# A gated delta rule in chunks of 128 frames: roots finished on GpSimd, the query's output part scaled out of PSUM, the identity by TensorE, Silu for the query, a tile of their own for the step sizes

## The chip, the cores and the metric

The kernel runs on one core of a Trainium2 chip. Five engines work side by side, each in the order of its own instruction list: PE (TensorE, matrix products), DVE (VectorE), ACT (ScalarE), POOL (GpSimd) and SP (SyncE, which issues transfers). An instruction that waits for a semaphore holds up all that stand behind it on its engine. The metric is the device time of one execution, in microseconds.

## The reference, cut to what matters

One layer of a streaming trunk: RMS norm, one input projection, a gated-delta-rule group of 4 heads (128 x 128 state each) beside an S5 state-space group, both gated, one output projection, a final norm. It runs on 4096 prompt frames from zero state and on 32 sample frames that continue a cache. What the change touches is the delta-rule group:

```python
    q = l2_normalize(q) * (DN_DK ** -0.5)        # q, k, v = silu(conv(h @ w_in))
    k = l2_normalize(k)                          # x * rsqrt(sum(x * x) + 1e-6)
    beta = sigmoid(b_logit)
    ...
    lower = where(strict, (k * beta) @ k.T * decay, 0.0) + eye     # one chunk of frames
    u = triangular_solve(lower, v * beta)
    w = triangular_solve(lower, k * beta * exp(gc))
    attn = where(incl, q @ k.T * decay, 0.0)
    ...
        v_new = u_b - w_b @ S                                      # the scan over chunks
        o = (q_b * exp(gc_b)) @ S + attn @ v_new
        S = S * exp(g_last) + (k_b * exp(g_last - gc_b)).T @ v_new
    ...
    o_dn = rms_norm(o_dn, dn_norm_w) * silu(z_dn)
```

`gc` is the running sum of the logarithm of the decay within a chunk, `beta` the step size.

## The kernel before

The time falls into stages. Up to some 690 us the kernel norms the frames, projects the S5 input, runs the S5 blocks and the gate projections, and makes the tables of decays. To 930 us it prepares weights and the first block of queries, keys and values. From there to some 2070 us it runs the delta rule beside the dense work of that stage, and from there to the end the output projection.

The delta-rule stage takes chunks of 128 frames, 32 of the prompt and one of the sample. PE's program is put together by a small planner (`Drive`): one stream of dense work (`qkv`, 256 frames at a time, line 1352 and around; then `s5out`) has the lowest priority, and four streams of chunks, `chunk(ci, ...)`, yield to one another and to it after each step with an estimate of how long the step's operands take. The lists of the other engines are then set by a scheduler that goes by estimated times, so each list is fixed before the kernel runs. A chunk's buffers carry the number of its stream, as in `br0` to `br3`, so that a buffer comes free with the end of the chunk four places before.

A chunk has three parts.

- The front, held by one chunk at a time (`busy`): PE transposes keys to rows, ACT squares them into `sk` (1522), POOL adds epsilon (1525), `rsqrt` makes the inverse root: a power on POOL (129), then one Newton step in three instructions on DVE (130 to 132), `rq_k` and `rqt_k`. ACT scales the keys to `kn` (1529). POOL makes `kd` from the keys and a table of decays (1546), multiplies the step sizes with the decay matrix, `br` times `dm` (1548), and the queries with `gr`, the exponential of `gc` for each frame (1550). `br` and `gr` come from DRAM, each frame's value repeated on all 128 partitions, by SP's transfers of lines 1510 and 1507. DVE scales the key products with `br` into `at` (1560) and the query products with `dm` (1571). `pair` splits a float32 tile into a float16 high half (ACT, 1482) and the rest (POOL or DVE, 1483), and `mm3` makes a product of two such pairs by three matmuls.
- The inverse of the triangular matrix (`inverse`, two slots): blocks of 4, 8, 16, 32 and 64 frames, `T`, `T64`, `Tf`, by small products on PE with DVE and ACT between them, then one residual correction: `e` is the identity less the product of matrix and `Tf` (1742, DVE), split into `eh` (1744, ACT) and `el` (1746, POOL).
- The chain through the state: `sp` (the state's pair), the corrected values `vn`, the output `po` as the sum of two products, query by state and attention by `vn`, in one PSUM bank, the state update `S_p` (1614, DVE), squares of `po` into `so` (1522, ACT; 1622, DVE), its inverse root `rq_o` with a factor `sdn` (1624), the gated output `o` from PSUM (1630, DVE, four heads), and its halves in `m16`, which lies in `dm` (1633, 1634).

In `qkv` the convolution is four multiplies into `acc` (1352 on ACT, 1354 on DVE); keys and values of all blocks but the first go through Silu (1356), queries through Tanh (1359) and (tanh + 1) times `acc` on DVE (1360).

## Time and profile before

| quantity | value |
| --- | --- |
| median of 3 runs | 2460.18 us (2457.91 to 2461.07) |
| profiled execution | 2456.1 us, its span 2454.4 us |
| PE busy in the span | 2080.0 us (85%) |
| DVE | 1578.9 us (64%) |
| ACT | 1204.6 us (49%) |
| POOL | 892.4 us (36%) |
| granted PE clock, mean | 0.937 |

The span is the part of the profiled execution from its first to its last instruction. The durations in the trace belong to that one execution. An engine is busy while an instruction runs on it; a wait is idle time and names the work that ended it.

### The profile page before, as it was taken

How to read it: one execution, taken by the hardware profiler on the slowest of the kernel's cores; microseconds unless marked ns; L12 is line 12 of the kernel's file. 1: busy time of each engine (PE TensorE's matmuls, PEld its weight loads, DVE VectorE, ACT ScalarE, POOL GpSimd, SP SyncE). 2: the span in 40 equal slices, each digit the busy share in tenths (PEclk: the TensorE clock that was granted, in tenths of full speed). 3: DMA queues.
4: the chain of work that ended last, by engine and by line, in shares of the span. 5: the costliest groups of instructions: out<-in, count | busy, mean ns of one | idle time of the engine just before them, and what ended most of it. 6: DMA issues, size and time to landing. Idle time of an engine off the chain costs nothing.

```text
span 2454.4 us, 47429 instructions
## 1 busy us (share of the span) xinstructions
PE 2080.0 (85%) x18040; PEld 1491.3 (61%) x18040; DVE 1578.9 (64%) x3715; ACT 1204.6 (49%) x3518; POOL 892.4 (36%) x1057
## 2 busy tenths in 40 slices
PE   3968898967799996986988789888878866999998
PEld 2635676734576554875777677777677743554443
DVE  3885766756474224886888778887878786642222
ACT  5457456423593113656666566666656564421101
POOL 1363011011102014556555555655655455420000
PEclk9989999979899997998999999999999888999999
DMA  5469877367864555231342233333333256455552
GB/s 164 152 165 248 164 164 183 67 75 104 233 174 125 116 123 112 57 80 40 79 83 69 62 66 85 76 83 76 62 58 58 58 143 123 117 142 155 152 146 90
DMA packets 458005, 278.05 MB, mean 113 GB/s; under 512 B 345112, under 2 KB 412928, under 8 KB 457264
## 3 DMA queue, kind: packets, MB, share of 16 engines
q1 hardware_dynamic: 435024, 206.94, 40.0%
q0 software_dynamic: 18000, 59.43, 7.3%
q10 hardware_dynamic: 4752, 8.65, 1.0%
q8 instruction: 141, 2.31, 0.4%
q14 instruction: 88, 0.72, 0.1%
HBM read 110.99 MB, written 86.23 MB: 80 GB/s over the span
## 4 chain that ended last, share of the span: by engine, by line
PE 32%; DVE 22%; DMA 15%; issue 14%; POOL 7%; ACT 6%; SPq 3%; POOLq 0%; DVEq 0%; ACTq 0%
PE pp L48 17%; PE pz L503 7%; DMA br<-be_d 6%; PE bk L48 4%; DVE acc L1354 3%; DMA gyt<-gy_d 2%; DMA h_d<-hl 2%; SPq L911 1%; DVE ubd L1687 1%; DMA gy_d<-vv 1%; DVE vv L879 1%; POOL br L1548 1%; PE bk L52 1%; PE pp L511 1%; DVE vv L885 1%
## 5 line engine op out<-in xcount | busy, mean ns | idle before, releaser
L503 PE MATMUL pz<-wz,hz 128*128 128x512 f16 (+1 forms) x1464 | 383.2, 388 | 20.3 <-DMA hz<-h_d 13.2
L1354 DVE SCALAR_TENSOR_TENSOR acc<-pp,cwu,acc 128x256 f32<-128x256 f32 x540 | 253.0, 475 | 39.1 <-ACT acc L1352 34.8
L48 PEld LDWEIGHTS <-mx 128*128 128x128 f16 (+1 forms) x1584 | 152.7, 98 | 178.8 <-issue 4.3
L503 PEld LDWEIGHTS <-hz 128*128 128x128 f16 (+1 forms) x1464 | 144.3, 100 | 179.2 <-issue 20.7
L48 PE MATMUL pp<-h,wk 128*128 128x259 f16 (+1 forms) x1632 | 224.6, 274 | 0.7 <-DVE gyt L1437 0.4
L48 PE MATMUL pp<-h,wv 128*128 128x259 f16 (+1 forms) x1632 | 220.3, 279 | 1.2 <-DVE acc L1354 1.2
L48 PE MATMUL pp<-h,wq 128*128 128x259 f16 (+1 forms) x1632 | 215.2, 275 | 1.3 <-DVE acc L1354 1.3
L511 PE MATMUL pp<-wa,ht 128*128 128x260 f16 x1536 | 189.8, 279 | 26.0 <-ACT wa L207 11.9
L48 PE MATMUL po<-wo,mx 128*128 128x512 f16 (+1 forms) x912 | 197.2, 379 | 0.3 <-ACT th L1184 0.3
L511 PEld LDWEIGHTS <-ht 128*128 128x128 f16 x1536 | 151.0, 100 | 52.8 <-issue 25.1
L48 PEld LDWEIGHTS <-wk 128*128 128x128 f16 x1632 | 155.1, 99 | 28.6 <-issue 3.6
L48 PEld LDWEIGHTS <-wv 128*128 128x128 f16 x1632 | 151.9, 101 | 33.4 <-issue 9.5
L48 PEld LDWEIGHTS <-wq 128*128 128x128 f16 x1632 | 151.6, 99 | 31.1 <-issue 9.5
L48 PE MATMUL pp<-wo,mx 128*128 128x512 f16 x672 | 153.9, 382 | 0.0
L537 POOL DMA_DIRECT2D z_d<-zt x64 | 36.7, 574 | 311.5 <-DVE zt L536 276.6
L48 PEld LDWEIGHTS <-a 128*128 128x128 f16 x1320 | 83.3, 102 | 89.1 <-issue 65.9
L536 DVE SCALAR_TENSOR_TENSOR zt<-zt,pz 128x512 f32<-128x512 f32 (+1 forms) x66 | 45.0, 682 | 134.7 <-ACT zt L535 134.5
L1522 ACT ACTIVATE jk<-bk 128x128 bf16<-128x128 f32 x396 | 109.9, 278 | 44.1 <-PE bk L52 32.5
L1548 POOL TENSOR_TENSOR br<-br,dm 128x512 f32<-128x512 f32 x33 | 42.4, 1284 | 196.9 <-DMA br<-be_d 137.0
L48 PE MATMUL pp<-wg,gh 128*128 128x512 f16 (+1 forms) x396 | 107.7, 403 | 6.0 <-DVE acc L1354 3.4
L1810 ACT ACTIVATE junk<-xt 128x1024 bf16<-128x1024 f32 (+1 forms) x19 | 20.1, 1056 | 176.4 <-issue 92.6
L1352 ACT ACTIVATE acc<-pp,cwu 128x256 f32<-128x256 f32 x180 | 85.1, 476 | 40.0 <-PE pp L48 26.9
(614 smaller groups left out, 4960.8 us busy)
## 6 DMA issues: line engine op xcount, KB each, us to landing
...
gy_d<-vv SPq DMA_DIRECT2D x128, 64.0 KB, 2.3
```

Source lines behind the costliest of these rows:

```text
L48: return self.nc.tensor.matmul(out, lhs, rhs, start=start, stop=stop)
L52: return self.nc.tensor.transpose(out, src, ident)
L503: self.nc.tensor.matmul(ps, a[x][:, c], w[:, y, c], start=c == 0 and x == y == 0, stop=c == K - 1 and x == 1)
L511: self.nc.tensor.matmul(pu[hf][:, :260], ht[x][:, c, :m], self.w_a[:, y, c, 260 * hf:260 * hf + 260], start=c == 0 and x == y == 0, stop=c ...
L536: nc.vector.scalar_tensor_tensor(zt, zt, 1.0, pz, op0=ALU.add, op1=ALU.mult)
L537: nc.gpsimd.dma_start(rows(dst[0][blk]) if blk >= 0 else dst[1], zt)
L879: v.tensor_tensor(vv, vv, rs, op=ALU.mult)
L885: v.tensor_tensor_scan(*(t.rearrange("p a m -> p (a m)") for t in (vv[:, ri], rt, a[:, ri])), 0.0, op0=ALU.mult, op1=ALU.add)
L1352: nc.scalar.activation(acc, ps[:, 0:n], AF.Copy, scale=cw[:, e, 0:1])
L1354: v.scalar_tensor_tensor(acc, ps[:, j:j + n], cw[:, e, j:j + 1], acc, op0=ALU.mult, op1=ALU.add)
L1522: act.activation(junk, src[:, h], AF.Square, accum_out=out[:, h:h + 1])
L1548: gp.tensor_tensor(br, br, dm, op=ALU.mult)
```

## The change

Five things change, nearly all of it in the delta-rule stage.

1. `rsqrt4` makes the power and the whole Newton step on POOL, five instructions. The addition into `so` and the scaling of `sk` for the queries go to POOL too, and the factor `sdn` goes into the Newton step (as `hdn`).
2. The table of exponentials by frame, its transfer to `gr`, and the queries' multiply and split with it are gone. The query by state product is made first, by itself, and ACT takes it out of PSUM with the frame's exponential as scale into `oa`, which lies in `br`; the attention product follows, and DVE adds it to `oa`. Squares and the gated output read `oa`.
3. In the residual, two more matmuls for each head add `Tf` and subtract the identity in PSUM; `eh` and `el` are read straight from PSUM, by ACT and DVE.
4. Queries of all blocks but the first go through Silu, and one ACT copy of the block (128 x 1024) applies their scale. The exponential of the tables is made once, behind them.
5. The step sizes have a tile of their own, `bl`, one for all streams, loaded for the next chunk as soon as the present chunk's multiply has read it. The diagonal is cleared in `br` on POOL instead of being set in `at`; `a32` goes from DVE to POOL, halves of `T64` and `Tf` from DVE to ACT, and `m16` from `dm` to `knT`.

```diff
+    def rsqrt4(self, x, tag, f):
+        gp = self.nc.gpsimd
...
+        gp.tensor_tensor(y, x, self.mhalf, op=ALU.pow)
+        gp.tensor_tensor(t, y, y, op=ALU.mult)
+        gp.tensor_tensor(t, t, x, op=ALU.mult)
+        gp.tensor_scalar(t, t, -3.0, -0.5 * f if isinstance(f, float) else f, op0=ALU.add, op1=ALU.mult)
+        gp.tensor_tensor(y, y, t, op=ALU.mult)
+        return y
...
+        self.last_exp = nc.scalar.activation(gcf, gcf, AF.Exp, scale=-1.0)
...
-                nc.scalar.activation(x, gc, AF.Exp)
-                nc.gpsimd.dma_start(self.eg_d[key].rearrange("h c t -> (h c) t"), x)
...
-                if b and nm != "q":
+                if b:
                     self.after(nc.scalar.activation(dst[:, h], acc, AF.Silu), self.last_exp)
...
+                    if b and nm == "q":
+                        nc.scalar.activation(dst, dst, AF.Copy, scale=self.sq["p"])
...
+    def load_be(self, ci):
+        self.bl = self.ck.tile([128, H, 128], F32, name="bl")
+        src = self.be_d["p"][:, ci] if ci < self.NC else self.be_d["s"][:, 0]
+        self.nc.sync.dma_start(self.bl, src.partition_broadcast(128))
...
-        gr = t4("gr")
-        cd = ci if key == "p" else 0
-        nc.sync.dma_start(gr, self.eg_d[key][:, cd].partition_broadcast(128))
         br = t4("br")
         dm = self.dms.pop(ci)
-        nc.sync.dma_start(br, self.be_d[key][:, cd].partition_broadcast(128))
...
-        rk = self.rsqrt(sk[:, 0], 128, H, "k")
+        rk = self.rsqrt4(sk[:, 0], "k", 1.0)
...
-        gp.tensor_tensor(br, br, dm, op=ALU.mult)
-        t = tmp()
-        gp.tensor_tensor(t[:, :, :m], qT[:, :, ts], gr[:, :, :m], op=ALU.mult)
...
-        qe = pair(gr, t)
+        gp.tensor_tensor(br, self.bl, dm, op=ALU.mult)
+        i = self.order.index(ci) + 1
+        if i < len(self.order):
+            self.load_be(self.order[i])
+        gp.affine_select(out=br, in_=br, pattern=[[0, H], [1, 128]], compare_op=ALU.not_equal, fill=0.0, base=0, channel_multiplier=-1)
...
-        v.tensor_scalar(sk[:, 1], sk[:, 1], self.eq[key], self.tau[key], op0=ALU.add, op1=ALU.mult)
+        gp.tensor_scalar(sk[:, 1], sk[:, 1], self.eq[key], self.tau[key], op0=ALU.add, op1=ALU.mult)
...
+        po = bk(self.po)
+        for h in range(H):
+            mm3(po[:, h], at_(qp, h), at_(sp, h))
         vn = pair(t4("knT"), pvn, v)
+        oa = t4("br")
+        for h in range(H):
+            act.activation(oa[:, h], po[:, h], AF.Copy, scale=self.ngC[:, h, ci:ci + 1])
         yield 2000
         po = bk(self.po)
         for h in range(H):
-            mm3(po[:, h], at_(qe, h), at_(sp, h), stop=False)
-            mm3(po[:, h], at_(aT, h), at_(vn, h), start=False)
+            mm3(po[:, h], at_(aT, h), at_(vn, h))
...
+        v.tensor_tensor(oa, oa, po, op=ALU.add)
         so = self.sm.tile([128, H], F32, name="so")
-        squares(po, so)
-        v.scalar_tensor_tensor(so, so, 1.0 / 128, sk[:, 1], op0=ALU.mult, op1=ALU.add)
-        ro = self.rsqrt(so, 128, H, "o")
-        v.tensor_scalar(ro, ro, self.sdn, None, op0=ALU.mult)
+        squares(oa, so)
+        gp.tensor_tensor(so, so, sk[:, 1], op=ALU.add)
+        ro = self.rsqrt4(so, "o", self.hdn)
...
-            v.scalar_tensor_tensor(o[:, h], po[:m, h], ro[:m, h:h + 1], zc[:m, h], op0=ALU.mult, op1=ALU.mult)
+            v.scalar_tensor_tensor(o[:, h], oa[:m, h], ro[:m, h:h + 1], zc[:m, h], op0=ALU.mult, op1=ALU.mult)
...
-        v.tensor_tensor(a32, at, hb(self.bd32), op=ALU.mult)
-        gp.affine_select(out=at, in_=at, pattern=[[0, H], [1, 128]], compare_op=ALU.not_equal, fill=1.0, base=0, channel_multiplier=-1)
+        gp.tensor_tensor(a32, at, hb(self.bd32), op=ALU.mult)
...
-        v.tensor_scalar(T64[:, :, 32:64], T, self.rsel[:, 1:2], None, op0=ALU.mult)
+        act.activation(T64[:, :, 32:64], T, AF.Copy, scale=self.rsel[:, 1:2])
...
-        v.tensor_scalar(Tf[:, :, 64:128], T64, self.rsel[:, 3:4], None, op0=ALU.mult)
+        act.activation(Tf[:, :, 64:128], T64, AF.Copy, scale=self.rsel[:, 3:4])
...
-            pe.mm(p[:, h], al[:, h], Tf[:, h], start=False, stop=True)
-        e = t4("br")
-        v.scalar_tensor_tensor(e, p, -1.0, hb(self.ident), op0=ALU.mult, op1=ALU.add)
+            pe.mm(p[:, h], al[:, h], Tf[:, h], start=False, stop=False)
+            pe.mm(p[:, h], ident16, Tf[:, h], start=False, stop=False)
+            pe.mm(p[:, h], ident16, self.nid16, start=False, stop=True)
         eh = i4("a4")
-        act.copy(eh, e)
+        act.activation(eh, p, AF.Copy, scale=-1.0)
         el = i4("a32")
-        gp.tensor_tensor(el, e, eh, op=ALU.subtract)
+        v.scalar_tensor_tensor(el, p, -1.0, eh, op0=ALU.mult, op1=ALU.subtract)
```

The lists of the engines change with it. In these listings a name's last number counts the tiles as they are made, so a larger one was made later. POOL of the kernel before, in the middle of the delta-rule stage, around the multiply of the step sizes of a chunk whose root has not come yet:

```order
L1627 DMA vb0_18332<-z_d1_88 128x512
L1548 TENSOR_TENSOR br0_18344<-br0_18344,dm_17996 128x512
L1525 TENSOR_SCALAR sk3_18037<-sk3_18037 128x4
L129 TENSOR_TENSOR rq_k_18049<-sk3_18037,mhalf_70 128x4
L1746 TENSOR_TENSOR a321_18359<-br1_18355,a41_18357 128x512
L1758 COPY br1_18520<-uf1_17895 128x512
L129 TENSOR_TENSOR rq_o_18325<-so_18318,mhalf_70 128x4
L1483 TENSOR_TENSOR sp_18606<-S_p_9211,sp_18606 128x512
L1546 TENSOR_TENSOR tp_18376<-kn3_18055,ed_7680 128x512
```

The multiply (line 1548) stands ahead of the addition and the power of another chunk's front (1525 and 129 with `rq_k`). In POOL's list of the changed kernel, at a like place a few chunks later:

```order
L132 TENSOR_TENSOR rqt_k_19833<-rq_k_19832 128x4
L1641 TENSOR_TENSOR so_20119<-so_20119,sk3_18010 128x4
L133 TENSOR_TENSOR rqt_k_19833<-rqt_k_19833,sk2_19820 128x4
L131 TENSOR_TENSOR rq_o_20126<-so_20119,mhalf_70 128x4
L134 TENSOR_SCALAR rqt_k_19833<-rqt_k_19833 128x4
L132 TENSOR_TENSOR rqt_o_20127<-rq_o_20126 128x4
L135 TENSOR_TENSOR rq_k_19832<-rq_k_19832,rqt_k_19833 128x4
L133 TENSOR_TENSOR rqt_o_20127<-rqt_o_20127,so_20119 128x4
L134 TENSOR_SCALAR rqt_o_20127<-rqt_o_20127,hdn_9166 128x4
L135 TENSOR_TENSOR rq_o_20126<-rq_o_20126,rqt_o_20127 128x4
L1560 TENSOR_TENSOR tp_20185<-kn2_19839,ed_7676 128x512
L1562 TENSOR_TENSOR br3_20144<-bl_20190,dm_19789 128x512
```

The roots of the front (`rqt_k`, `rq_k`) and of an older chunk (`so`, `rq_o`) stand between one another, with one power (131) and four small instructions (132 to 135) each; the split of the state (1501 with `sp`) stands directly ahead of these, between the front's power and its next step, and the multiply by the step sizes (1562), which reads `bl`, stands behind them all.

DVE of the kernel before, at the place of the first listing; `th` and `acc` are a query block's Tanh and convolution:

```order
L1360 SCALAR_TENSOR_TENSOR qT_18262<-th_18554,acc_18549 128x256
L1687 TENSOR_TENSOR ubd0_18150<-us0_18148,bd32_9266 128x512
L1360 SCALAR_TENSOR_TENSOR qT_18262<-th_18626,acc_18621 128x256
L130 SCALAR_TENSOR_TENSOR rqt_k_18050<-rq_k_18049 128x4
L1614 SCALAR_TENSOR_TENSOR S_p_9211<-S_p_9211,egl_7681,bk_18301 128x128 x4
L131 TENSOR_TENSOR rqt_k_18050<-rqt_k_18050,sk3_18037 128x4
L1354 SCALAR_TENSOR_TENSOR acc_18727<-pp_18668,cwu_8629,acc_18727 128x256
L1622 SCALAR_TENSOR_TENSOR so_18318<-so_18318,sk0_16218 128x4
L132 SCALAR_TENSOR_TENSOR rq_k_18049<-rqt_k_18050,rq_k_18049 128x4
```

The state update (1614) stands behind the first step of the front's root (130). DVE of the changed kernel, around a state update and the gated output of one chunk:

```order
L1632 SCALAR_TENSOR_TENSOR S_p_9196<-S_p_9196,egl_7677,bk_23143 128x128 x2
L1365 SCALAR_TENSOR_TENSOR acc_23598<-pp_23556,cwu_8626,acc_23598 128x256
L1365 SCALAR_TENSOR_TENSOR acc_23550<-pp_23460,cwu_8626,acc_23550 128x256
L1716 TENSOR_TENSOR T0_23213<-T0_23079,bk_23208 128x128
L1365 SCALAR_TENSOR_TENSOR acc_23598<-pp_23556,cwu_8626,acc_23598 128x256
L1701 STREAM_TRANSPOSE us0_23215<-T0_23213 128x128
L1703 TENSOR_TENSOR ubd0_23217<-us0_23215,bd32_9248 128x512
L1365 SCALAR_TENSOR_TENSOR acc_23697<-pp_23614,cwu_8626,acc_23697 128x256
L1762 SCALAR_TENSOR_TENSOR a321_23206<-bk_23187,a41_23204 128x512
L1365 SCALAR_TENSOR_TENSOR acc_23697<-pp_23614,cwu_8626,acc_23697 128x256 x2
L1712 TENSOR_TENSOR p10_23265<-bk_23260,lm16_9269 128x128
L1648 SCALAR_TENSOR_TENSOR kn0_23177<-br0_23060,rq_o_23168,vb0_23175 128x128 x4
```

No step of a root is left in the list; the gated output (1648) now follows from `br0`, the sum in SBUF, and from `rq_o`, which POOL makes, and inverse steps of another chunk (1712, 1716) stand on either side of it.

## Rows read from the trace of the kernel before

**Rows 1.** The page: the chain that ended last, its share of the span by line.

```profile
PE pp L48 17%; PE pz L503 7%; DMA br<-be_d 6%; PE bk L48 4%; DVE acc L1354 3%; DMA gyt<-gy_d 2%; DMA h_d<-hl 2%; SPq L911 1%; DVE ubd L1687 1%; DMA gy_d<-vv 1%; DVE vv L879 1%; POOL br L1548 1%; PE bk L52 1%; PE pp L511 1%; DVE vv L885 1%
```

**Rows 2.** Window, its us, busy us (count) of PE, PEld, DVE, ACT, POOL; clock, DMA, GB/s.

```profile
1000.00:2000.00 1000.00, 842.27 (x9299) 712.24 (x9299) 815.81 (x1997) 609.99 (x1934) 578.19 (x601) 0.94 0.32 72
```

**Rows 3.** Timeline from 1445 us: start, duration, engine, line, out<-in [idle before <-releaser].

```profile
1445.93 0.83 PE L48 MATMUL bk<-knT 128*128 128x128 f16 x12
...
1454.94 0.37 SPq L1510 DMA_DIRECT2D br<-be_d  x1
...
1456.36 0.66 PE L52 MATMUL bk<-ident,kT 128*128 128x128 f32 x4
...
1461.57 0.22 ACT L1522 ACTIVATION_READ_ACCUMULATOR jk<-bk 128x1 f32 x1
...
1463.31 1.26 POOL L1548 TENSOR_TENSOR br<-br,dm 128x512 f32<-128x512 f32 x1 [8.62 <-PE bk L48]
...
1464.96 1.04 POOL L129 TENSOR_TENSOR rq_k<-sk,mhalf 128x4 f32<-128x4 f32 x1
...
1466.03 1.12 DVE L130 SCALAR_TENSOR_TENSOR rqt_k<-rq_k 128x4 f32<-128x4 f32 x1 [5.25 <-POOL rq_k L129]
...
1467.07 1.11 DVE L1614 SCALAR_TENSOR_TENSOR S_p<-S_p,egl,bk 128x128 f32<-128x128 f32 x4
...
1468.57 0.15 DVE L1622 SCALAR_TENSOR_TENSOR so<-so,sk 128x4 f32<-128x4 f32 x1
...
1468.89 0.26 PE L48 MATMUL bk<-sp,knT 128*128 128x128 f16 x1 [3.90 <-ACT sp L1482]
```

**Rows 4.** As rows 2, the two microseconds after PE resumed.

```profile
1470.00:1472.00 2.00, 2.00 (x15) 1.70 (x13) 2.00 (x6) 1.39 (x5) 2.00 (x2) 0.50 0.00 0
```

**Rows 5.** Waits, 1000 to 2000 us: us in total, times, longest.

```profile
POOL br L1548 <- DMA br<-be_d: 128.8, 18, 9.8
DVE rqt_k L130 <- POOL rq_k L129: 87.3, 24, 6.2
PE bk L48 <- DVE T L1681: 28.3, 24, 5.8
```

**Rows 6.** Busy time of DVE on the tiles rqt_k, then rqt_o, 1000 to 2000 us.

```profile
1000.00:2000.00 1000.00, 29.61 (x84) 0.94 0.32 72
1000.00:2000.00 1000.00, 44.01 (x81) 0.94 0.32 72
```

**Rows 7.** DVE lines there: busy us, mean ns; then ns min/median/max of two lines.

```profile
L1360 DVE SCALAR_TENSOR_TENSOR qT<-th,acc 128x256 f32<-128x256 f32 x54 | 43.3, 823 | 14.6 <-PE bk L48 8.5 <-PE bk L52 4.7 <-ACT th L1359 1.3
L1654 DVE TENSOR_TENSOR a<-br,bd 128x512 f16<-128x512 f32 x28 | 20.1, 718 | 0.0
L1714 DVE TENSOR_SCALAR T<-T,rsel 128x128 f16<-128x128 f16 x28 | 20.1, 719 | 0.0
L1728 DVE TENSOR_SCALAR Tf<-T,rsel 128x256 f16<-128x256 f16 x28 | 18.3, 655 | 0.2
...
L1714 DVE TENSOR_SCALAR T<-T,rsel x28: 203/619/2020, 1020.3 to 1981.4; 128x128 f16<-128x128 f16 x28
L1630 DVE SCALAR_TENSOR_TENSOR kn<-bk,rq_o,vb x108: 303/338/353, 1040.7 to 1981.0; 128x128 f32<-128x128 f32 x104, 32x128 f32<-32x128 f32 x4
```

**Rows 8.** POOL lines there, by shape: busy us, mean ns.

```profile
L1550 POOL TENSOR_TENSOR tp<-qT,gr 128x512 f32<-128x512 f32 x27 | 35.1, 1301 | 0.0
L1746 POOL TENSOR_TENSOR a<-br,a 128x512 f16<-128x512 f32 x28 | 32.8, 1172 | 10.6 <-ACT a L1744 10.6
L1525 POOL TENSOR_SCALAR sk<-sk 128x4 f32<-128x4 f32 x28 | 6.6, 235 | 10.1 <-ACT jk L1522 8.1
```

**Rows 9.** ACT lines there, by shape: busy us, mean ns.

```profile
L1482 ACT CAST gr<-tp 128x512 f16<-128x512 f32 x28 | 17.7, 632 | 0.6 <-POOL tp L1550 0.5
L1538 ACT ACTIVATE vb<-bk,hbC 128x128 f32<-128x128 f32 x112 | 32.0, 371 | 5.3 <-PE bk L52 4.0 <-DVE bk L1497 1.2
```

**Rows 10.** ACT table loads of one line, whole span: busy us, mean ns.

```profile
L975 ACT ACT_TABLE_LOAD x2 | 2.6, 1283 | 0.0
```

More of the change, by code (lines that the diff above doesn't have):

```diff
@@ L102, in __init__ @@
         nc.vector.tensor_copy(self.ident16, self.ident)
+        self.nid16 = c.tile([128, 128], F16, name="nid16")
+        nc.vector.tensor_single_scalar(self.nid16, self.ident, -1.0, op=ALU.mult)
         self.h_d = [self.dram.tile([2, 1024, 1024], F16, name=f"h_d{b}") for b in range(T // 1024)]
@@ L352, in phase_a @@
                 self.table(ci)
+        gcf = self.ngC.rearrange("t h c -> t (h c)")
+        mark = self.last_exp
+        self.last_exp = nc.scalar.activation(gcf, gcf, AF.Exp, scale=-1.0)
+        self.after(self.last_exp, mark)
         self.phase_b1()
@@ L1032, in scales @@
         self.em = mm[:, 2:3]
-        self.sdn = cst.tile([128, 1], F32, name="sdn")
+        self.hdn = cst.tile([128, 1], F32, name="hdn")
         self.ss5 = cst.tile([128, 1], F32, name="ss5")
-        v.tensor_scalar(self.sdn, un["zd"], mm[:, 3:4], 2.0 ** 14, op0=ALU.mult, op1=ALU.mult)
+        v.tensor_scalar(self.hdn, un["zd"], mm[:, 3:4], -(2.0 ** 16.5), op0=ALU.mult, op1=ALU.mult)
         v.tensor_scalar(self.ss5, un["zs"], mm[:, 3:4], 2.0 ** 13, op0=ALU.mult, op1=ALU.mult)
@@ L1063, in ready @@
             nc.vector.tensor_scalar(cwu[:, sl], cw[:, sl], self.un[nm], None, op0=ALU.mult)
-            nc.vector.tensor_single_scalar(self.cwh[:, sl], cwu[:, sl], 1.0 if nm == "q" else 0.5, op=ALU.mult)
+            nc.vector.tensor_single_scalar(self.cwh[:, sl], cwu[:, sl], 0.5, op=ALU.mult)
             self.wq.append(w)
@@ L1137, in phase_b @@
         self.dms, self.sdone = {}, False
+        self.order = [i[0] for i in items]
+        self.load_be(self.order[0])
         for i in items[:NP]:
@@ L1234, in bounds @@
         for i, key in ((0, "p"), (2, "s")):
-            t = wt.tile([128, 6], F32, name=f"sg_{key}")
+            t = wt.tile([128, 5], F32, name=f"sg_{key}")
             v.tensor_single_scalar(t[:, 0:1], inv[:, i:i + 1], 2.0 ** 11, op=ALU.mult)
             v.tensor_single_scalar(t[:, 1:2], inv[:, i + 1:i + 2], 2.0 ** 8, op=ALU.mult)
-            v.scalar_tensor_tensor(t[:, 2:3], t[:, 1:2], 128 * EPS, t[:, 1:2], op0=ALU.mult, op1=ALU.mult)
-            v.scalar_tensor_tensor(t[:, 4:5], t[:, 0:1], 4e-6, t[:, 0:1], op0=ALU.mult, op1=ALU.mult)
+            v.scalar_tensor_tensor(t[:, 2:3], t[:, 1:2], 128 * 128 * EPS, t[:, 1:2], op0=ALU.mult, op1=ALU.mult)
+            v.scalar_tensor_tensor(t[:, 4:5], t[:, 0:1], 1e-6 if key == "p" else 4e-6, t[:, 0:1], op0=ALU.mult, op1=ALU.mult)
             v.tensor_single_scalar(t[:, 3:4], e[:, i + 1:i + 2], 2.0 ** -8, op=ALU.mult)
-            v.tensor_single_scalar(t[:, 5:6], e[:, i:i + 1], 2.0 ** -12, op=ALU.mult)
-            if key == "p":
-                self.hsq = t[:, 5:6]
             self.sq[key], self.eq[key], self.tau[key], self.usv[key] = t[:, 0:1], t[:, 4:5], t[:, 2:3], t[:, 3:4]
@@ L1292, in masks @@
             self.lm[b] = t
-        self.ist = wt.tile([128, 32], F32, name="ist")
+        self.ist16 = wt.tile([128, 32], F16, name="ist16")
         for q in range(4):
-            nc.vector.tensor_copy(self.ist[32 * q:32 * q + 32], self.ident[32 * q:32 * q + 32, 32 * q:32 * q + 32])
-        self.ist16 = wt.tile([128, 32], F16, name="ist16")
-        nc.vector.tensor_copy(self.ist16, self.ist)
+            nc.vector.tensor_copy(self.ist16[32 * q:32 * q + 32], self.ident[32 * q:32 * q + 32, 32 * q:32 * q + 32])
         self.rsel = wt.tile([128, 4], F32, name="rsel")
@@ L1354, in qkv @@
                     v.scalar_tensor_tensor(acc, ps[:, j:j + n], cw[:, e, j:j + 1], acc, op0=ALU.mult, op1=ALU.add)
-                if b and nm != "q":
+                if b:
                     self.after(nc.scalar.activation(dst[:, h], acc, AF.Silu), self.last_exp)
                 else:
-                    th = wk.tile([128, 256], F32, name="th", bufs=2)
-                    m0 = nc.scalar.activation(th, acc, AF.Tanh, scale=self.hsq if b else 0.5 if nm == "q" else 1.0)
-                    m1 = v.scalar_tensor_tensor(dst[:, h], th, 1.0, acc, op0=ALU.add, op1=ALU.mult)
+                    m0 = nc.scalar.activation(dst[:, h], acc, AF.Tanh)
+                    m1 = v.scalar_tensor_tensor(dst[:, h], dst[:, h], 1.0, acc, op0=ALU.add, op1=ALU.mult)
                     self.marks.append((m0, m1))
                 if h == H - 1:
+                    if b and nm == "q":
+                        nc.scalar.activation(dst, dst, AF.Copy, scale=self.sq["p"])
                     self.blk[b, nm] = dst
@@ L1562, in chunk @@
         yield 1400
-        qp = tmp()
+        qp = t4("gr")
         if m < 128:
@@ L1680, in inverse @@
             T = st("T", bufs=2)
-            v.tensor_tensor(T, hb(self.ist), p, op=ALU.subtract)
+            v.tensor_tensor(T, hb(self.ist16), p, op=ALU.subtract)
         def expand(T, nm):
```

11 lines of the change are left out of this document (4 added, 7 removed).

## The prediction

> **What bounds the kernel now.** I read five views in this order: the chain that ended last, the busy time of the engines in the chunk stage, one stall in order of time, the waits of the stage, and then the price of each touched line.
>
> The chain by line [rows 1] is led by PE's projections (lines 48 and 503), but the first thing on it that is not work of an engine is the transfer `br<-be_d`, 6% of 2454.4 us, some 147 us. The busy times of 1000 to 2000 us [rows 2], 28 chunks by the counts of its lines, give the balance of one chunk: 1000/28 = 35.7 us, in which PE is busy 842.27/28 = 30.1 us, DVE 815.81/28 = 29.1, ACT 609.99/28 = 21.8 and POOL 578.19/28 = 20.7. PE is nearest to full and idle for 157.7 us, 5.6 a chunk. What ends those 5.6 us decides.
>
> One stall in order of time [rows 3]. PE transposes the front chunk's keys at 1456.36. SP has issued the step-size transfer only at 1454.94, and POOL's `br` multiply starts at 1463.31, 8.4 us later. POOL runs its list in order, and the multiply stands ahead of the front chunk's root, so `rq_k` starts at 1464.96 and DVE, whose list has the root's next step ahead of the state update `S_p`, starts `rqt_k` at 1466.03 after 5.25 us of idleness. The state update follows at 1467.07, and PE, which had nothing else left, resumes at 1468.89 after 3.90 us. It then runs at half clock: 0.50 in 1470 to 1472 [rows 4], which is the 1.2 GHz level, after those idle microseconds. The waits say how often: POOL waits 128.8 us on that transfer, DVE 87.3 us on `rq_k` in 24 chunks, 87.3/28 = 3.1 us a chunk, and PE 28.3 us on the inverse's `T` from DVE [rows 5]. So over half of PE's idle time is one transfer that starts too late, passed on through two lists that are run in order.
>
> **The change part by part.** All prices are per chunk.
>
> *Own room for step sizes.* The transfer now goes into `bl`, and is issued right behind the previous chunk's multiply. That is about one interval of 35.7 us ahead of its own multiply, against 8.4 + 1.26 = 9.7 us of transfer and multiply [rows 3]. It is covered as long as two fronts are over 9.7 us apart. At the start four fronts come close together, and there it isn't: c1 to c3 may each wait up to 9.7 us, while the second block's projections stand beside them; I take 0 there, 10 us either way. On SP's list the transfer now waits for POOL's multiply where it waited for PE's product of the chunk four places before; the loads of `dm` and of the dense stream stand behind it as they did. POOL's list no longer has the multiply ahead of the root (the lists shown above). What is late next: the root is now nine POOL instructions, with the older chunk's state split and its `so` among them.
>
> *Newton steps on POOL.* DVE loses the three small steps of each root: 29.61 and 44.01 us in the window [rows 6], 73.6/28 = 2.6 us. The norm's multiply by `sdn` goes, at the mean of an `rqt_o` operation 44.01/81 = 0.54, and the additions of `so` and `sk`, between the 0.15 of `so` in [rows 3] and 0.54; I take 0.6 for both. POOL gains ten small operations. The nearest row is its 128x4 addition, 0.235 us [rows 8], so 2.4 us; the upper end is the power in `rq_k`, 1.04 us [rows 3], so 10.4. The ten are additions and multiplications, so I take 2.4.
>
> *Query.* Two scalar_tensor_tensors per chunk leave DVE, 43.3/28 = 1.55 us [rows 7]. ACT's Tanh becomes a Silu of the same shape, at nothing, and it gains half a copy of 128x1024, priced as one 128x512 cast, 0.63 [rows 9].
>
> *Output part.* POOL loses the query's decay multiply, 35.1/28 = 1.25, and a low half of the size of 1.17 [rows 8]; ACT loses the cast of `gr`, 0.63 [rows 9]; SP loses a broadcast transfer. ACT gains four evacuations with a scale, as line 1538: 32.0/28 = 1.14 [rows 9]. DVE gains one 128x512 addition with an operand in PSUM, 0.72 by line 1654 [rows 7]. The evacuations stand beside PE's second output product, but the addition now stands between the last product and the root: it makes the norm later by some 0.7 us and nothing else.
>
> *Residual.* Eight more f16 128x128 matmuls on PE: twelve took 0.83 us [rows 3], so 0.55, on the engine that is nearest to full. The cast and the low half now both read PSUM; POOL loses 1.17 [rows 8], and DVE's instruction keeps its shape, at nothing.
>
> *Small moves.* DVE's `a32` (0.72), `T64` (0.72) and `Tf` (0.65) halves leave [rows 7]; POOL gains `a32` at the price of the decay multiply, 1.25, ACT two copies between 0.29 and 0.63 each [rows 9], 0.75 for both. Of ACT's table loads four go, 1.28 us each [rows 10]: between nothing and 5.1 us once, by how many of them stand on the path of the S5 stage; I take 2.
>
> The sums. DVE: 2.6 + 0.5 + 0.6 + 1.55 + 0.7 + 0.7 + 0.65 - 0.7 = 6.6 less, 29.1 to 22.5. POOL: 1.25 + 1.17 + 1.17 - 1.25 - 2.4, unchanged at 20.7. ACT: 0.63 + 1.14 + 0.75 - 0.63 = 1.9 more, to 23.7. PE: 30.1 + 0.55 before the clock.
>
> PE's idle 5.6 then loses the 3.1 that DVE waited for `rq_k`, and 2.5 are left. Of these 28.3/28 = 1.0 are waits for `T`, which stands in DVE's list behind other work; with DVE at 22.5 of 32 us instead of 29.1 of 35.7 (70% against 82%) I take 0.3 off. I add 0.2 for a new wait: the four `o` instructions stand in DVE's list and wait there for POOL's `rq_o`, with the inverse's `T` behind them. So 2.4, a gain of 3.2. The clock averages 0.94 [rows 2], about 6% of 30.1 = 1.8 us lost; with the stall gone I leave 0.6 lost, a gain of 1.2. Less 0.55 for the matmuls: 3.2 + 1.2 - 0.55 = 3.85 us, times 28 chunks = 108, with the table loads 110. The profiled execution took 2456.1 us, so 2346; it lies 4.1 below the median of the three runs, so the median should be **2350 us**.
>
> Bounds. All of the idle time and of the clock's loss gone: (5.6 + 1.8 - 0.55) x 28 = 192, 2268. Half of the 3.1 gone and 0.5 of the clock: (1.55 + 0.5 - 0.55) x 28 = 42, 2418.
>
> *A rule against part of this.* The `o` instructions, which read PSUM and took 303 to 353 ns, now read their product from SBUF; the move of line 1714, which has all of its operands there, took 203 ns at the least, 619 in the middle and 2020 at the most [rows 7]. By the Trainium skill, "SBUF — State Buffer", section "SBUF: two separate sides", VectorE and GpSimd share a pair of SBUF ports that one of them holds for a whole instruction, which a VectorE instruction with two SBUF inputs wants as well. By that rule, which the spread of line 1714 agrees with, the four would take up to 0.42 us more each, DVE would stand at 24.2 instead of 22.5, and I would leave the 0.3 out: 8 us, an estimated 2358.
>
> **The rivals.**
>
> *A. The stall changes its place.* The key's root stands on POOL behind the older chunk's state split and `so`, and ACT's `kn` waits for all of it. For: in [rows 3] the older chunk's squares end at 1461.8, 5.4 us after the transposes, and the state split waits for a state update on DVE; so the root could end 10 us after the transposes instead of 12. Against: nothing on POOL then waits for memory. PE's idle falls by only 1.0, the clock's loss by 0.4: (1.0 + 0.4 - 0.55) x 28 = 24, about **2436**.
>
> *B. Slower.* The same place, but the state split on POOL waits for the state update, which DVE holds behind an `o` that waits for POOL's `rq_o`: a ring of lists in order. It decides against the change where the front's product reaches PE later than now, 12.5 us behind the key's transposes (1456.36 to 1468.89) [rows 3]. Equal to now it costs the matmuls, 0.55 x 28 = 15 us; each microsecond beyond costs 28. At half a microsecond it gives **2490**. Against it: what POOL waited on was 8.4 us of a transfer, and the ten small operations come to 2.4. Only at the power's price, 10.4, would they take its place.
>
> *C. PE to the full.* DVE's relief frees the waits for `T` too, and PE idles 1.0 us with 0.4 lost on the clock: (4.6 + 1.4 - 0.55) x 28 = 153, **2305**. For: PE's leading share [rows 1]. Against: the inverse is a chain of small steps between three engines.
>
> *D. The change doesn't do what it says:* `bl` is one buffer, so a multiply that runs late holds up the next transfer. Where fronts lie within 9.7 us of one another the old wait is back. At one interval in three it leaves (3.85 x 2/3) x 28 = 72 us, about **2388**, inside the forecast's bounds.
>
> **How the numbers follow.** The forecast has 0.55 (2268 to 2418 at its outer bounds), A 0.20, C 0.12, B 0.10, D 0.03. The range 2290 to 2440 takes in the forecast, D and most of A, and half of C; what is left out is B, the quicker half of C and A's upper edge, under 2 in 10. This kernel's measurement tells 0.2%, 4.9 us, from no change. Faster by more: the forecast, C, D and nearly all of A, 0.86. Within: 0.05, from A's end. Slower: B, 0.09.
>
> **What would show it.** Right: in the changed kernel's waits POOL's `br` multiply no longer waits for a transfer outside the start, DVE shows no wait for `rq_k`, the busy times per chunk are about 22.5 (DVE), 20.7 (POOL), 23.7 (ACT), the interval is near 31.9 us and the granted clock 0.98. Wrong by A or B: ACT's `kn` or POOL's state split leads the waits, and the clock stays at 0.94. Wrong in a price: a small POOL operation far above 0.235 us, or PE's stage busy above 30 us a chunk at a full clock.

## The result and the profile after

The changed kernel takes 2366.71 us, median of 4 runs (2359.84 to 2371.43), against 2460.41 us for the kernel before beside it (4 runs, 2457.91 to 2461.07): a ratio of 0.9618, with a 95% interval of 0.9604 to 0.9632. A second measurement of the same two kernels gave 0.9655 (0.9640 to 0.9671). The forecast was 2350 us in a range of 2290 to 2440. The profiled execution took 2359.84 us.

The page of the changed kernel, its busy times, then the chain by line, and the busy times of the same stretch as [rows 2], with the same columns:

```profile
PE 2057.6 (87%) x18304; PEld 1492.6 (63%) x18304; DVE 1436.9 (61%) x3289; ACT 1246.6 (53%) x3693; POOL 895.3 (38%) x1318
...
PE pp L48 23%; PE pz L521 8%; PE bk L48 7%; PE bk L52 2%; DMA gyt<-gy_d 2%; ACT jk L1536 2%; DVE acc L1365 1%; PE pt L1028 1%; SPq L929 1%; DVE vv L897 1%; DMA gy_d<-vv 1%; DVE vv L903 1%; PE pp L529 1%; DMA hz<-h_d 1%; DMA bl<-be_d 1%
```

```profile
1000.00:2000.00 1000.00, 903.64 (x10319) 771.20 (x10319) 765.45 (x1794) 719.72 (x2305) 641.07 (x895) 0.96 0.31 76
```

The step-size transfer, 6% of the chain in [rows 1], is down to 1% (`bl<-be_d`). In the stretch 31 chunks now run instead of 28 (counted, as for [rows 2], by a line of the inverse that runs once a chunk), 1000/31 = 32.3 us each. Per chunk PE is busy 29.2 us, DVE 24.7, ACT 23.2 and POOL 20.7, and PE idles 3.1 us instead of 5.6.

The waits of 1000 to 2000 us, us in total, times and longest, which answer to [rows 5]:

```profile
POOL br L1562 <- DVE kn L1648: 21.4, 21, 1.8
...
PE bk L48 <- DVE T L1697: 19.2, 21, 7.1
...
ACT kn L1543 <- POOL rq_k L135: 10.6, 17, 1.1
...
DVE kn L1648 <- POOL rq_o L135: 7.7, 10, 2.1
```

And the line of before that stands against the third of them:

```profile
ACT kn L1529 <- DVE rq_k L132: 36.0, 18, 5.3
```

Neither of the two waits that led in [rows 5] is left. POOL's multiply waits 21.4 us for a reader of the buffer and no longer for a transfer. DVE's list has no step of the root any more, so that it has no wait for `rq_k` says little by itself; but the front's keys, which wait for the root in both kernels, do so for 10.6 us instead of 36.0. The new wait, `o` for `rq_o`, comes to 7.7 us.

A front of the changed kernel, to be held against [rows 3] (start, duration, engine, line, out<-in, idle time before):

```profile
1435.18 0.66 PE L52 MATMUL bk<-ident,kT 128*128 128x128 f32 x4
```

```profile
1436.89 1.15 POOL L1501 TENSOR_TENSOR sp<-S_p,sp 128x512 f16<-128x512 f32 x1 [1.30 <-ACT sp L1500]
...
1438.44 1.04 POOL L131 TENSOR_TENSOR rq_k<-sk,mhalf 128x4 f32<-128x4 f32 x1
...
1440.01 0.20 POOL L132 TENSOR_TENSOR rqt_k<-rq_k 128x4 f32<-128x4 f32 x1
...
1442.50 0.20 POOL L135 TENSOR_TENSOR rq_k<-rq_k,rqt_k 128x4 f32<-128x4 f32 x1
...
1448.15 1.28 POOL L1562 TENSOR_TENSOR br<-bl,dm 128x512 f32<-128x512 f32 x1 [1.01 <-DVE kn L1648]
```

```profile
1437.68 0.19 ACT L1536 ACTIVATION_READ_ACCUMULATOR jk<-bk 128x1 f32 x1
...
1444.75 1.14 ACT L1543 ACTIVATE kn<-bk,rq_k 128x128 f32<-128x128 f32 x4
```

From the transposes of the keys at 1435.18 it is 9.6 us to `kn`; at the place of [rows 3] it was 12.75 (1456.36 to 1469.11). Over all 28 fronts from c4 on the median is 7.9 us, and was 12.0. What went is the time between ACT's last square of the keys and POOL's addition, the first step of the root on POOL: 4.4 us in the median of these fronts before, 0.1 us after. The state split (line 1501 with `sp`) stands ahead of the root, as rival A had it, but it ends at 1438.04, 0.2 us after the last square (1437.87), so POOL's part of it costs the front next to nothing here. The multiply at 1448.15 stands behind all of it.

**Where the 96 us are.** A mark that means the same in both kernels is ACT's scaling of the front's keys, `kn`. It starts for chunk c4 at 1116.13 before and at 1136.90 after, for the last chunk at 2111.31 and 2004.40. That cuts either trace in three: the start from 930 us, the 27 intervals between, and the end. The windows of before, then of after (the window's us, then busy us and count of PE, PEld, DVE, ACT and POOL, the granted clock, DMA share, GB/s):

```profile
930.00:1116.13 186.13, 150.00 (x1681) 124.28 (x1681) 132.14 (x315) 100.36 (x318) 97.53 (x110) 0.89 0.38 83
1116.13:2111.31 995.18, 823.93 (x8839) 677.95 (x8839) 787.84 (x1914) 595.50 (x1873) 567.61 (x585) 0.92 0.35 78
2111.31:2454.40 343.09, 331.35 (x1835) 160.09 (x1833) 130.38 (x247) 64.50 (x150) 51.59 (x67) 0.99 0.48 134
```

```profile
930.00:1136.90 206.90, 165.19 (x1822) 132.39 (x1821) 119.31 (x275) 110.41 (x351) 102.81 (x149) 0.91 0.33 69
1136.90:2004.40 867.50, 786.45 (x8951) 669.85 (x8951) 666.68 (x1552) 626.51 (x2004) 571.55 (x797) 0.95 0.32 78
2004.40:2358.00 353.60, 341.83 (x1897) 165.61 (x1895) 127.52 (x231) 70.28 (x166) 48.02 (x80) 0.99 0.50 138
```

The 27 intervals fell from 995.2 to 867.5 us, 127.7 us, or 36.9 to 32.1 each. The start grew by 20.8 us and the end by 10.5, and 127.7 - 20.8 - 10.5 = 96.4 us is the difference of the two spans. But the marks cut off unequal amounts of work, so these three numbers are not gains and losses. In the end PE is busy for 341.8 of 353.6 us; 42 products of the output projection (`pp<-wo,mx`) that stood in the 27 intervals before (144 there, now 102) stand behind them now, 8.4 us of PE's time. In the start PE has 1822 products instead of 1681.

PE's idle time tells the two apart. Up to 930 us it is 165.8 us after and was 155.3 before, 10.5 more. In the start it is 206.9 - 165.2 = 41.7 and was 186.1 - 150.0 = 36.1, 5.6 more. In the intervals it is 81.1 and was 171.3, 90.2 less. In the end it is 11.8 and was 11.7. Together that is 74 us less, and PE is busy for 22.4 us less, 2057.6 against 2080.0, which makes the 96.4 us. So the intervals won 90.2 us of idle time, and 16.1 were lost ahead of them.

Of the 10.5 us up to 930, most stands in one wait, PE's for the operand of the gate projections. Before, then after:

```profile
PE pz L503 <- DMA hz<-h_d: 13.2, 9, 5.0
```

```profile
PE pz L521 <- DMA hz<-h_d: 20.4, 11, 4.9
```

The last of these projections starts at 930.27 before and at 942.53 after, so 12 of the 20.8 us were there before the chunks began. The changed kernel's second trace (e9) has 21.7 us of this wait, and e1 and e2, which are the kernel before with small edits, 10.3 and 13.1. What in the change makes these transfers later was not tried.

The start has one stall that was not there before. POOL, then ACT, then PE of the changed kernel:

```profile
959.38 1.05 POOL L131 TENSOR_TENSOR rq_k<-sk,mhalf 128x4 f32<-128x4 f32 x1
...
967.71 1.26 POOL L1562 TENSOR_TENSOR br<-bl,dm 128x512 f32<-128x512 f32 x1 [7.08 <-DMA bl<-be_d]
...
969.18 0.20 POOL L132 TENSOR_TENSOR rqt_k<-rq_k 128x4 f32<-128x4 f32 x1
...
978.15 1.26 POOL L1562 TENSOR_TENSOR br<-bl,dm 128x512 f32<-128x512 f32 x1 [7.48 <-DMA bl<-be_d]
979.37 0.20 POOL L135 TENSOR_TENSOR rq_k<-rq_k,rqt_k 128x4 f32<-128x4 f32 x1
```

```profile
979.61 1.14 ACT L1543 ACTIVATE kn<-bk,rq_k 128x128 f32<-128x128 f32 x4 [8.96 <-POOL rq_k L135]
```

```profile
970.27 1.04 PE L52 MATMUL pp<-ident,gyt 128*32 128x128 f32 x4 [12.70 <-POOL gyt L1433]
```

The root of chunk c0 begins at 959.38 and ends with its last instruction at 979.37. Between its five instructions stand the multiplies of c1 and c2, and each waits over 7 us for `bl`, which is loaded for one chunk at a time. `kn` of c0 so starts at 979.61, where it was at 940.88 before, and PE waits 12.70 us for a copy on POOL (line 1433, the S5 output of the sample) that is queued behind the same multiply. It looks like the old stall, now at the start only. Two runs below have no queue on `bl` there, and c4 is as late in them: see e4 and e8.

### The profile page after: what moved, and what is told of

It reads as the page before. It is cut to its first block, busy times and chain, and to the rows that moved or that the text cites. A ratio compares the mean times of both kernels' runs of the same rounds, so it can differ in the third digit from the quotient of the medians.

```text
span 2358.0 us, 47816 instructions
## 1 busy us (share of the span) xinstructions
PE 2057.6 (87%) x18304; PEld 1492.6 (63%) x18304; DVE 1436.9 (61%) x3289; ACT 1246.6 (53%) x3693; POOL 895.3 (38%) x1318
## 4 chain that ended last, share of the span: by engine, by line
PE 43%; issue 12%; DVE 11%; DMA 10%; ACT 7%; POOL 4%; SPq 2%; DVEq 0%; POOLq 0%; ACTq 0%
PE pp L48 23%; PE pz L521 8%; PE bk L48 7%; PE bk L52 2%; DMA gyt<-gy_d 2%; ACT jk L1536 2%; DVE acc L1365 1%; PE pt L1028 1%; SPq L929 1%; DVE vv L897 1%; DMA gy_d<-vv 1%; DVE vv L903 1%; PE pp L529 1%; DMA hz<-h_d 1%; DMA bl<-be_d 1%
## 5 line engine op out<-in xcount | busy, mean ns | idle before, releaser
L48 PE MATMUL pp<-h,wv 128*128 128x259 f16 (+1 forms) x1632 | 208.9, 271 | 0.3 <-DVE acc L1365 0.3
L48 PEld LDWEIGHTS <-a 128*128 128x128 f16 x1320 | 77.8, 98 | 38.6 <-issue 28.7
L1825 DVE SCALAR_TENSOR_TENSOR xt<-po,uo,xt 128x512 f32<-128x512 f32 (+1 forms) x38 | 28.4, 748 | 116.7 <-PE po L48 116.6
```

Source lines behind the costliest of these rows:

```text
L48: return self.nc.tensor.matmul(out, lhs, rhs, start=start, stop=stop)
L1825: v.scalar_tensor_tensor(xt[:m, sl], ps, self.uo[:m], xt[:m, sl], op0=ALU.mult, op1=ALU.add)
```

## The experiments

All ratios are to the kernel before, run beside on the same chip, with 95% intervals. The first question was whether the late transfer or DVE's load held PE.

**e1: no transfer of the step sizes.**

```diff
-        nc.sync.dma_start(br, self.be_d[key][:, cd].partition_broadcast(128))
...
-        gp.tensor_tensor(br, br, dm, op=ALU.mult)
+        gp.tensor_tensor(br, dm, dm, op=ALU.mult)
```

> The kernel before, with the transfer of the step sizes left out and the multiply of line 1548 squaring dm instead: the step sizes are left out of the result, all else is as before, and POOL's multiply still stands ahead of the front's root. Theory (the late transfer is the stall): the 3.1 us a chunk that DVE waited for rq_k and some 0.8 us of half clock go, 28 x 3.9 = 109 us, so about 2352 us (2335 to 2390). Rival (DVE's load is what holds PE): at most 20 us, 2440 or more, since DVE does the same work.

Measured 2364.33 us, 0.958 (0.9553 to 0.9607). Two lines away, and the whole gain of the change is there. Its window and the wait for the root's end:

```profile
1000.00:2000.00 1000.00, 883.40 (x9824) 739.80 (x9822) 884.83 (x2132) 661.85 (x2074) 622.02 (x650) 0.95 0.30 76
```

```profile
ACT kn L1528 <- DVE rq_k L132: 13.4, 11, 5.9
```

DVE is busy for 884.8 of 1000 us, more than in [rows 2], and PE for 883.4. DVE's load was not what held PE. The wait of DVE for `rq_k`, 87.3 us in [rows 5], is no longer among the 60 longest. The run takes the transfer away altogether, so it doesn't tell a late transfer from any transfer; e3 does.

**e2: Silu alone.**

```diff
...
-                if b and nm != "q":
+                if b:
                     self.after(nc.scalar.activation(dst[:, h], acc, AF.Silu), self.last_exp)
                 else:
-                    th = wk.tile([128, 256], F32, name="th", bufs=2)
...
+                    if b and nm == "q":
+                        nc.scalar.activation(dst, dst, AF.Copy, scale=self.sq["p"])
```

> The kernel before with the query through Silu and one ACT copy for its scale, nothing else. Theory (stall): DVE loses 1.55 us a chunk but still waits for the transfer, 2445 to 2460 us. Rival (DVE's load): 1.55 of the 6.6 us that the whole change takes off DVE, so 1.55/6.6 x 94 = 22 us, about 2438 us.

Measured 2452.72 us, 0.9929 (0.9914 to 0.9945), some 17 us less than the 2469.37 us of the kernel before on that chip. The ratio lies between the two expectations. Its waits:

```profile
POOL br L1546 <- DMA br<-be_d: 159.7, 22, 8.9
...
DVE rqt_k L130 <- POOL rq_k L129: 77.7, 24, 5.8
```

Both waits of [rows 5] are there, 159.7 and 77.7 us. The stall stays where only DVE is relieved.

**e3: Silu, and own room for the step sizes.** As e2, and besides:

```diff
...
+    def load_be(self, ci):
+        self.bl = self.ck.tile([128, H, 128], F32, name="bl")
+        src = self.be_d["p"][:, ci] if ci < self.NC else self.be_d["s"][:, 0]
+        self.nc.sync.dma_start(self.bl, src.partition_broadcast(128))
...
-        nc.sync.dma_start(br, self.be_d[key][:, cd].partition_broadcast(128))
...
-        gp.tensor_tensor(br, br, dm, op=ALU.mult)
+        gp.tensor_tensor(br, self.bl, dm, op=ALU.mult)
+        i = self.order.index(ci) + 1
+        if i < len(self.order):
+            self.load_be(self.order[i])
```

> As the run with Silu alone, and the step sizes in a tile of their own, loaded behind the previous chunk's multiply (the room comes from the Tanh's tile that Silu frees). POOL's multiply still stands ahead of the front's root in most chunks. Theory (stall): most of the gain, 2350 to 2385 us, and no wait of POOL for that transfer outside the first chunks. Rival (DVE's load): as Silu alone, 2430 to 2440 us. Second rival (the order of POOL's list, not the transfer): some 2400 us or more, since the order is that of before.

Measured 2383.7 us, 0.9652 (0.9637 to 0.9667): 69 us less than e2, as the first theory had it.

```profile
DVE rqt_k L130 <- POOL rq_k L129: 5.9, 10, 1.7
```

POOL's multiply stands ahead of the root of the chunk before it in 31 of 32 places, as in the kernel before, but no wait of POOL for a transfer is among the 60 longest, and DVE waits 5.9 us for `rq_k` instead of 77.7 in e2. So POOL's order alone did no harm; the order together with a late transfer did.

**e4: the changed kernel with the late transfer.**

```diff
...
         br = t4("br")
         dm = self.dms.pop(ci)
+        nc.sync.dma_start(br, self.be_d[key][:, ci if key == "p" else 0].partition_broadcast(128))
...
-        gp.tensor_tensor(br, self.bl, dm, op=ALU.mult)
-        i = self.order.index(ci) + 1
-        if i < len(self.order):
-            self.load_be(self.order[i])
+        gp.tensor_tensor(br, br, dm, op=ALU.mult)
...
-        oa = t4("br")
+        oa = t4("gr")
```

> The changed kernel with the step sizes loaded into the chunk's own br again, at the place of before (oa then lies in gr), all its other parts kept. POOL's multiply stands ahead of the front's root again. Theory (stall): the stall is back, some 3 us a chunk, 2366 + 28 x 3 = 2450 us (2430 to 2475). Rival (DVE's load): 2366 to 2390 us, since DVE is relieved as in the changed kernel.

Measured 2479.14 us, 1.0039 (1.0022 to 1.0056): slower than before, just beyond the theory's 2475.

```profile
1000.00:2000.00 1000.00, 852.12 (x9487) 736.87 (x9488) 674.71 (x1621) 642.83 (x2059) 559.68 (x797) 0.92 0.25 60
```

```profile
POOL br L1562 <- DMA br<-be_d: 128.4, 16, 9.6
ACT kn L1543 <- POOL rq_k L135: 118.5, 26, 7.8
```

POOL waits 128.4 us for the transfer, as in [rows 5], and ACT 118.5 us for the root. From ACT's last square of the keys to POOL's addition it is 6.4 us in the median. DVE is busy for 674.7 us, against 815.81 in [rows 2], and it helps nothing. With e1 and e3 this settles the main cause from both sides.

The same run settles less of the start. It has no `bl`, and no multiply of the first four chunks waits over 1.8 us for its transfer. Yet PE waits for the copy of the sample as before, the start has PE's idle time of the changed kernel (206.94 - 165.55 = 41.4 us), and `kn` of c4 comes at the same time:

```profile
972.18 1.04 PE L52 MATMUL pp<-ident,gyt 128*32 128x128 f32 x4 [14.65 <-POOL gyt L1432]
```

```profile
930.00:1136.94 206.94, 165.55 (x1814) 132.32 (x1812) 122.24 (x271) 108.53 (x342) 102.24 (x148) 0.90 0.31 70
```

```profile
1136.94 1.14 ACT L1543 ACTIVATE kn<-bk,rq_k 128x128 f32<-128x128 f32 x4 [6.71 <-POOL rq_k L135]
```

So c4 does not come late for the queue on `bl` alone. What else holds the copy and the start back was not tried by itself.

The second question was what the other parts are worth. Each of the next four undoes one of them, or mends the start.

**e5: the Newton steps on DVE.** In `rsqrt4` the four instructions behind the power go to `nc.vector`:

```diff
-        gp.tensor_tensor(t, y, y, op=ALU.mult)
+        v.tensor_tensor(t, y, y, op=ALU.mult)
...
```

> The changed kernel with the four small steps of both roots on DVE instead of POOL, all else kept. Ratio to the kernel before; the changed kernel has 0.9618. Theory (the transfer was the stall, DVE's load is not what holds PE any more): within 0.3% of the changed kernel, 0.961 to 0.965. Rival (DVE's load): DVE gets back some 2.6 us a chunk, 2.6/6.6 of what the parts beside the step sizes could give, and o waits for steps in DVE's list: 0.970 or more. Second rival: better than the changed kernel, below 0.960, since POOL's list gets shorter by 2.4 us a chunk and the root ends sooner.

Measured 2379.37 us, 0.9656 (0.9635 to 0.9677): between the theory's 0.965 and the rival's 0.970, and too near the first to be told from it.

**e6: no matmuls for the identity.**

```diff
-            pe.mm(p[:, h], al[:, h], Tf[:, h], start=False, stop=False)
-            pe.mm(p[:, h], ident16, Tf[:, h], start=False, stop=False)
-            pe.mm(p[:, h], ident16, self.nid16, start=False, stop=True)
+            pe.mm(p[:, h], al[:, h], Tf[:, h], start=False, stop=True)
```

> The changed kernel without the eight matmuls of the identity and of Tf (the residual is then not the reference's; that part is left out). Theory (PE is near its full load, so each matmul counts): 8 x 0.069 us x 33 = 18 us less, 0.9545 (0.951 to 0.957). Rival (they lie in PE's idle time): within 0.2% of 0.9618.

Measured 2380.26 us, 0.9665 (0.9645 to 0.9685): slower with less work, which neither expectation had.

**e7: the query through Tanh again.**

```diff
-                if b:
+                if b and nm != "q":
                     self.after(nc.scalar.activation(dst[:, h], acc, AF.Silu), self.last_exp)
+                elif b:
+                    self.after(nc.scalar.activation(dst[:, h], acc, AF.Tanh, scale=0.5), self.last_exp)
+                    v.scalar_tensor_tensor(dst[:, h], dst[:, h], 1.0, acc, op0=ALU.add, op1=ALU.mult)
```

> The changed kernel with the query through Tanh and (tanh + 1) times acc on DVE again, written in place; the copy with the query's scale stays on ACT. DVE gets 1.55 us a chunk back. In the kernel before, Silu alone brought 0.7%. Theory (that 0.7% came from the stall: a DVE list that is behind after it): here only 0.1 to 0.3% more than 0.9618, 0.963 to 0.965. Rival (DVE's load counts by itself): 0.968 to 0.970.

The query comes out doubled, which its normalisation takes out again. Measured 2351.48 us, 0.955 (0.9528 to 0.9573): faster with more work on DVE, a miss again.

**e8: the first four chunks' step sizes loaded apart.**

```diff
...
+        i = self.order.index(ci)
+        if i < NP:
+            nc.sync.dma_start(br, self.be_d[key][:, ci].partition_broadcast(128))
+        if i == NP - 1:
+            self.load_be(self.order[NP])
...
+        gp.tensor_tensor(br, self.bl if i > NP else br, dm, op=ALU.mult)
+        if NP < i < len(self.order):
             self.load_be(self.order[i])
```

> The changed kernel with the step sizes of the first four chunks loaded into their own br as before, and the tile bl loaded from the fifth on, so that the first four multiplies don't wait 9.7 us for one another. Theory (PE's idle time of 33.7 us between 930 us and the fifth multiply, 25.4 before, comes from that): 8 us less, 0.9585. Rival (the fifth chunk waits for the dense work, not for the first four): within 0.1% of 0.9618.

Measured 2392.56 us, 0.971 (0.9687 to 0.9734), slower than the changed kernel. The start is not mended: `kn` of c4 comes at 1137.65 (1136.90 without the edit). PE still waits for the copy on POOL:

```profile
PE pp L52 <- POOL gyt L1432: 15.8, 1, 15.8
```

The scheduler had put all four multiplies ahead of c0's root and of that copy, though none of them waits over 1.6 us. PE's idle time in the start does fall, to 207.65 - 170.44 = 37.2 us, but PE has more products there and c4 is no earlier:

```profile
930.00:1137.65 207.65, 170.44 (x1867) 135.78 (x1864) 120.03 (x276) 111.39 (x351) 103.67 (x150) 0.91 0.33 73
```

With e4's 41.4 us, what the queue on `bl` costs the start lies between nothing and some 5 us. And the chunks behind c4, whose work the edit doesn't touch, took longer, (2050.82 - 1137.65)/27 = 33.8 us each instead of 32.1.

An edit at the start that slows the middle points to the lists. Of the 1318 instructions of POOL's list, 210 stand elsewhere than in the changed kernel's sequence in e8, and 212 in e6: the scheduler sets every list anew for every edit. So the last question was what an order alone is worth.

**e9 to e12: the changed kernel again, the planner's factor at 1.4 and at 1.6, and e7 again, side by side.**

```diff
-SLACK = 1.5
+SLACK = 1.4
```

> The changed kernel itself, beside the runs below on one chip: 0.962 (0.960 to 0.964).

> The changed kernel with the planner's factor on its estimates at 1.4 instead of 1.5: the same instructions, in another order on every engine. Theory (after the step sizes, what is left between the versions is the order of the lists): off the changed kernel by 0.3 to 1% to either side. Rival (order matters little, and the single parts made the differences between the last four runs): within 0.2% of 0.962.

> As the run before with 1.6. Theory: off by 0.3 to 1% to either side. Rival: within 0.2% of 0.962.

> The changed kernel with the query through Tanh and DVE again, beside the changed kernel itself. If its lead holds, 0.955 (0.953 to 0.957), 0.7% below the changed kernel; if it came from the other chip, 0.962.

| kernel | median, us | ratio | interval |
| --- | --- | --- | --- |
| e9, the changed kernel | 2379.58 | 0.9655 | 0.9640 to 0.9671 |
| e10, factor 1.4 | 2387.47 | 0.9681 | 0.9659 to 0.9703 |
| e11, factor 1.6 | 2363.8 | 0.9588 | 0.9571 to 0.9605 |
| e12, Tanh | 2354.87 | 0.9549 | 0.9532 to 0.9566 |

e9 has the changed kernel's lists row by row and came out 0.15% above the range that was expected of it. e10 and e11 have the same instructions in another order, and gave 0.3% more and 0.7% less than e9. The windows of 1140 to 1900 us, of e10, e11 and e12 in this order:

```profile
1140.00:1900.00 760.00, 688.81 (x7984) 598.39 (x7984) 588.36 (x1370) 543.45 (x1740) 488.38 (x692) 0.96 0.29 67
```

```profile
1140.00:1900.00 760.00, 706.49 (x8227) 615.53 (x8226) 573.42 (x1406) 557.76 (x1801) 500.83 (x708) 0.97 0.30 69
```

```profile
1140.00:1900.00 760.00, 701.08 (x8320) 611.80 (x8320) 610.53 (x1476) 564.81 (x1821) 504.87 (x716) 0.98 0.31 72
```

e10 and e11 do the same work, but in 760 us PE is busy for 688.8 us in the one and 706.5 in the other. By this measure e3, e5 and e6 can't be told from the changed kernel: 0.9652, 0.9656 and 0.9665 lie within what a new order does to 0.9618 to 0.9655. e12 is 1.1% faster than the changed kernel beside it and kept its 0.955 on two chips, so it is the fastest version here; whether it owes that to the Tanh or to its order stays open, as e11 comes within 0.4% of it with Silu.

## Why the prediction was right, point by point

**The stall.** Right. The two waits are gone, with the transfer alone (e1, e3), and back with it (e4). Fronts from the transposes to `kn` fell from 12.0 to 7.9 us, so rivals A and B, which had the stall on POOL and ACT again, were wrong: the state split does stand ahead of the root, but the root starts 0.1 us behind the keys' squares in the median.

**The terms of a chunk.** In the stretch of [rows 2]: the interval 31.9 foretold, 32.3 measured. PE's busy time 30.1 + 0.55 - 1.2 = 29.5 foretold, 29.2 measured. Idle 2.4 foretold, 3.1 measured. Clock 0.98 foretold, 0.96 measured. ACT 23.7 and 23.2, POOL 20.7 and 20.7. That stretch takes in the slow start of the changed kernel, up to 1136.90.

Between the marks of `kn` PE's idle time fell by 90.2/27 = 3.3 us an interval, 3.2 foretold, so the main term was right in mechanism and size. For PE's busy time 1.2 - 0.55 = 0.65 us a chunk stood, 18.2 for 28 chunks, and over the whole span it is 22.4 less, with the matmuls of the identity in it. How much of that the clock gave back and how much the matmuls cost is open, since e6, made for that, came out with other lists.

**The small operations on POOL.** Taken at 0.235 us, 2.4 for ten, measured there (busy us, mean ns):

```profile
L1590 POOL TENSOR_SCALAR sk<-sk,sg_p 128x4 f32<-128x4 f32 x31 | 11.8, 380 | 32.9 <-ACT jk L1536 32.6
...
L134 POOL TENSOR_SCALAR rqt_o<-rqt_o,hdn 128x4 f32<-128x4 f32 x29 | 8.3, 286 | 2.7
...
L135 POOL TENSOR_TENSOR rq_k<-rq_k,rqt_k 128x4 f32<-128x4 f32 x31 | 6.8, 221 | 0.9
```

The means of the ten lie between 202 and 380 ns and come to 2.4 us a chunk; the power's 1.04 us was no price for them.

**DVE.** 22.5 foretold, 24.7 measured: mis-sized. The gated output and the inverse's first product, in the same stretch (ns min/median/max):

```profile
L1648 DVE SCALAR_TENSOR_TENSOR kn<-br,rq_o,vb x116: 298/344/1283, 1066.7 to 1978.0; 128x128 f32<-128x128 f32 x112, 32x128 f32<-32x128 f32 x4
```

```profile
L1670 DVE TENSOR_TENSOR a<-br,bd x31: 682/1135/1648, 1021.1 to 1983.2; 128x512 f16<-128x512 f32 x31
```

With their operand in PSUM the `o` instructions took 303 to 353 ns [rows 7]; with both in SBUF the median is 344 but the longest took 1283, and the mean is 470 ns in place of 339. The first product, 721 ns in the mean before, has a median of 1135 and a mean of 1158; it now runs beside `a32` on POOL, which reads the same tile. Line 1451 of the dense stream (1439 before), also with two operands in SBUF, went from 791 to 1158 ns. These three make some 1.3 of the 2.2 us a chunk that DVE lies above the forecast.

The Trainium skill, "SBUF — State Buffer", section "SBUF: two separate sides", has VectorE with two SBUF inputs and GpSimd exclude one another on a shared pair of ports; these rows agree. The 24.2 us that the paragraph on the rule had is the nearer figure, but in part by luck: it had 0.42 us for each `o`, where 0.13 was measured, and nothing for the other two.

PE hardly waited for it: DVE has 32.3 - 24.7 = 7.6 us a chunk to spare, and PE's waits for `T` fell from 28.3 to 19.2 us.

**The start and the stage before it.** For the start 0 stood, 10 us either way, for the waits of c1 to c3 on `bl`. They came as foretold (7.08, 7.48 and, for c3, 6.32 us of POOL's time). PE's idle time grew by 5.6 us there, within the 10; e4 has nearly all of that without these waits and e8 has 4.5 us less than the changed kernel, so how much of it is theirs stays open. What the sum had no term for is the stage before: 10.5 us more of PE's idle time up to 930 us, its transfers of `hz` above all, where only a gain of 2 from the table loads stood. Nothing of those 2 us can be seen.

**The sum.** Foretold: 3.2 x 28 = 89.6 of idle time, 18.2 of busy time and 2, together 110. Measured: 90.2 and 22.4, less 5.6 and 10.5 ahead of the intervals, 96.4 as the spans have it. So the two main terms came out 5 us above their forecast, and 16 us were lost where the sum had a gain of 2. The forecast of 2350 came within 17 us of 2366.7 because its main terms held; that the loss ahead of the chunks, for which it had no term, was no larger is luck.
